# Seven quarter products for eight in two token-major products, and operand tiles at multiples of 512 bytes

## The chip, the core and the metric

The kernel runs on one core of one Trainium2 chip. Its time is the device time of one execution in microseconds; the median of the runs counts. TensorE (PE) does the matmuls, VectorE (DVE), ScalarE (ACT) and GpSimd (POOL) the elementwise work, and SyncE's queue (SP) issues nearly all DMAs.

## The reference

A trunk of two layers on 512 tokens of 1024 channels, in float32. Cut to what matters here:

```python
h = x
# layer 0: gMLP mixer
z = gelu(rmsnorm(h, g0) @ w_in)          # 1024 -> 4096
u, v = split(z)                          # 2048 columns each
s = spatial_mix(layernorm(v)) + b        # over tokens, in chunks of 128
h = h + (u * s) @ w_out
h = h + (silu(conv(hn @ w_gate)) * (hn @ w_up)) @ w_down
# layer 1: forgetting attention, 16 heads of 64
q, k, v, f = split(rmsnorm(h, g1) @ w_qkvf)
h = h + attention(q, k, v, cumsum(log_sigmoid(f + b_f))) @ w_o
h = h + (silu(conv(hn @ w_gate)) * (hn @ w_up)) @ w_down
out = rmsnorm(h, g_final)
```

The change concerns `v` of layer 0 (1024 by 2048 weights) and `v` of layer 1 (1024 by 1024).

## The kernel before

Every float32 product is made of three matmuls on halves: each operand is split into a rounded high half and the rest, and `triple` (L163 to L169) adds high by high, high by low and low by high into one PSUM bank. The residual stream `h` lies in SBUF channel-major, eight tiles of 128 channels by 512 tokens. `norm_split` makes the halves `xh`, `xl` of the scaled `h` of each tile (ACT L126, DVE L127); `norm_square` squares it on ACT and adds the squares up on GpSimd (L140, L141). The RMS factor per token is applied to the product's result, so a product may begin before the factor is there.

Weights stream in units of 128 by 1024 (512 KB) through SP's queue into `raw` (three buffers). For each unit ACT casts the high half `whi` (L112) and DVE subtracts to get the low half `wlo` (L113), two buffers each; `unit` and `fetch` keep two units ahead.

Two kinds of product use them. `gemm_fm` (channel-major output) takes weights as the stationary operand, 24 matmuls of 512 columns per unit. `gemm_tm` (L187 to L206, token-major output) has token blocks of x stationary and the weights moving: per group of 512 output columns four banks, four units, 24 matmuls of 512 columns per unit. In `gmlp` it makes v in four groups; the GELU (ACT L248) reads the banks, and `bn_stats` (DVE L249) follows. In `fox` it makes V in two groups, scaled into halves from the banks (L385, L386). `norm_end`, `norm_spread`, `gates`, `running_sums` and `spatial` hang on points inside these products.

At the start the first unit comes in two halves and x in quarters and then pairs of tiles, all on SP's queue, with `norm_split` of each pair behind it. The output products of gMLP and of both FFNs have products' inputs `z` (halves in 32 tiles); the down product's evacuation `add_to_h` (L210 to L220) adds four banks to `h`, splits them and squares them. The order on each engine is set by the tile framework's scheduler, from the order in which the code is written, its dependencies and its own cost table.

## Time and profile before

| | us |
|---|---|
| median of 3 runs | 1096.44 (1095.24 to 1096.6) |
| the profiled execution | 1095.16 |
| its span | 1093.4, granted clock 0.998 |
| PE busy | 1075.3 (98%) |
| DVE busy | 620.2 (57%) |
| ACT busy | 440.7 (40%) |
| POOL busy | 67.3 (6%) |

The span runs from the first to the last instruction; the profiled execution's own time is 1.8 us longer. Busy shares are means over the stages. In order of time these are: v product (5.14 to 101.84 us), u product (to 203.36), gMLP output (to 291.35), first FFN (to 467.34) and its down product (to 555.25), fox V (to 608.19), QK and attention, fox output, second FFN, and the last down product from 995.68.

### The profile page before, as it was taken

What the parts mean: (1) busy time and instruction counts of PE and PEld (TensorE: products, weight loads), DVE (VectorE), ACT (ScalarE), POOL (GpSimd) and SP (SyncE); (2) the same over time, 40 slices, a digit from 0 to 9 for tenths busy, and PEclk for the clock granted to TensorE, in tenths of its full rate; (3) what the DMA queues carried; (4) which work ended last, traced back from release to release, by engine and by line L of the source; (5) the groups of instructions that cost most, each with busy time, mean ns of one, the idle gap of its engine ahead of it and who ended that gap; (6) DMA issues with size and microseconds to landing.
All of it is one profiled execution on the core that took longest, in us unless ns stands there. A gap on an engine that the chain in (4) does not pass through costs nothing. (4 is left out here: it accounts for less than half of the span.)

```text
span 1093.4 us, 12918 instructions
## 1 busy us (share of the span) xinstructions
PE 1075.3 (98%) x5018; PEld 882.4 (81%) x5018; DVE 620.2 (57%) x1007; ACT 440.7 (40%) x706; POOL 67.3 (6%) x62
## 2 busy tenths in 40 slices
PE   7999999999999999999999999999999999999997
PEld 6878888888888888888887787777778888888886
DVE  5435856524555665545255588898665656655232
ACT  5332333323333433333133577777542433432232
POOL 6000000001200000001020000000021000000000
PEclk9999999999999999999999999999999999999999
DMA  6322222222222222222222211211222222232222
GB/s 237 109 84 97 86 89 78 86 95 96 90 95 97 97 97 97 97 97 97 97 97 81 81 61 44 77 40 53 84 77 97 97 97 96 82 111 87 89 95 77
DMA packets 28957, 99.44 MB, mean 91 GB/s; under 512 B 3488, under 2 KB 4256, under 8 KB 28896
## 3 DMA queue, kind: packets, MB, share of 16 engines
q1 hardware_dynamic: 28752, 98.52, 26.1%
q8 instruction: 39, 0.64, 0.2%
q14 instruction: 22, 0.18, 0.1%
q10 hardware_dynamic: 144, 0.10, 0.0%
HBM read 96.12 MB, written 2.10 MB: 90 GB/s over the span
## 5 line engine op out<-in xcount | busy, mean ns | idle before, releaser
L113 DVE TENSOR_TENSOR wlo<-raw,whi 128x1024 fp32r<-128x1024 f32 (+1 forms) x173 | 217.0, 1255 | 377.9 <-ACT whi L112 365.5
L112 ACT CAST whi<-raw 128x1024 fp32r<-128x1024 f32 (+1 forms) x173 | 180.8, 1045 | 457.9 <-PE psg L168 123.7
L167 PE MATMUL psg<-x,whi 128*128 128x512 f32 x336 | 136.6, 407 | 0.0
L169 PE MATMUL psg<-x,wlo 128*128 128x512 f32 x336 | 131.4, 391 | 0.0
L168 PE MATMUL psg<-x,whi 128*128 128x512 f32 x336 | 130.9, 390 | 0.0
L167 PE MATMUL pss<-x,whi 128*128 128x512 f32 x208 | 81.8, 393 | 0.0
L169 PE MATMUL pss<-x,wlo 128*128 128x512 f32 x208 | 81.0, 389 | 0.0
L168 PE MATMUL pss<-x,whi 128*128 128x512 f32 x208 | 80.9, 389 | 0.0
L169 PEld LDWEIGHTS psg<-x,wlo 128*128 128x128 f32 x336 | 63.1, 188 | 13.7
L167 PEld LDWEIGHTS psg<-x,whi 128*128 128x128 f32 x336 | 64.1, 191 | 11.2 <-issue 0.2
L168 PEld LDWEIGHTS psg<-x,whi 128*128 128x128 f32 x336 | 63.3, 188 | 11.4 <-issue 0.2
L141 POOL TENSOR_TENSOR tmp<-tmp,tmp 128x512 f32<-128x512 f32 x28 | 45.1, 1612 | 402.7 <-ACT tmp L140 401.2
L167 PE MATMUL psg<-z,whi 128*128 128x512 f32 x128 | 50.7, 397 | 0.0
L169 PE MATMUL psg<-z,wlo 128*128 128x512 f32 x128 | 50.3, 393 | 0.0
L168 PE MATMUL psg<-z,whi 128*128 128x512 f32 x128 | 49.9, 390 | 0.0
L168 PEld LDWEIGHTS pss<-x,whi 128*128 128x128 f32 x208 | 39.1, 188 | 8.2 <-issue 0.2
L169 PEld LDWEIGHTS pss<-x,wlo 128*128 128x128 f32 x208 | 39.0, 188 | 8.2
L167 PEld LDWEIGHTS pss<-x,whi 128*128 128x128 f32 x208 | 39.1, 188 | 8.1 <-issue 0.2
L167 PE MATMUL psa<-x,whi 128*128 128x512 f32 x112 | 44.1, 394 | 0.0
L169 PE MATMUL psb<-x,wlo 128*128 128x512 f32 x112 | 43.6, 389 | 0.0
L168 PE MATMUL psa<-x,whi 128*128 128x512 f32 x112 | 43.6, 389 | 0.0
L167 PE MATMUL psb<-x,whi 128*128 128x512 f32 x112 | 43.6, 389 | 0.0
(283 smaller groups left out, 2233.2 us busy)
## 6 DMA issues: line engine op xcount, KB each, us to landing
raw<-w SPq DMA_DIRECT2D x175, 512.0 KB
out<-v SPq DMA_DIRECT2D x8, 256.0 KB
h<-x SPq DMA_DIRECT2D x3, 512.0 KB
raw<-w SPq DMA_DIRECT2D x2, 256.0 KB
h<-x SPq DMA_DIRECT2D x4, 128.0 KB
pt<-ws SPq DMA_DIRECT2D x1, 512.0 KB
pt<-bs SPq DMA_DIRECT2D x1, 512.0 KB
z<-cum SPq DMA_DIRECT2D x32, 8.0 KB
```

The lines of the kernel that those rows point to most:

```text
L112: nc.scalar.copy(out=hi, in_=src)
L113: nc.vector.tensor_tensor(out=lo, in0=src, in1=hi.bitcast(F32), op=ALU.subtract)
L141: nc.gpsimd.tensor_tensor(out=self.acc, in0=self.acc, in1=sq, op=ALU.add)
L167: self.nc.tensor.matmul(out, ah, bh, start=start, stop=False)
L168: self.nc.tensor.matmul(out, ah, bl, start=False, stop=False)
L169: self.nc.tensor.matmul(out, al, bh, start=False, stop=stop)
```

## The change

It brings in a class `Seven`: one step of a Strassen-Winograd scheme. For a group of 512 output columns, x is cut into halves of channels (even and odd tiles, `k = 2q` and `2q + 1`) and of tokens (0 to 255, 256 to 511), the weights into four quarters 11, 12, 21, 22 of one unit each. Instead of eight quarter products there are seven, numbered 1 to 7: 1 and 2 take plain quarters of x and of the weights; 5, 6 and 7 take sums `S` of x quarters and differences of weight quarters; 4 takes a plain quarter of x with a difference, 3 takes a sum with quarter 22. One product is 24 matmuls of 256 columns into one bank (two token blocks, four `q`, three matmuls).

Around it: `sums` makes the S of one q (ACT scales h, DVE three subtractions and one combined operation of 256 columns each, then halves of four quarters); `diff` makes weight differences on DVE, 128 by 1024, four per group; `product` adds the seven results up into output quarters in SBUF (DVE, and an ACT copy for product 1). For a plain quarter with `added` (seven times in gMLP, twice in fox) the low half is not subtracted by DVE: ACT writes the negated high half, and a DMA issued by GpSimd adds the weights to it from memory. The GELU and fox's scaling read SBUF instead of the bank. gMLP runs 28 products, fox 14. Groups 0 and 1 are interleaved by `START`. In fox, the sums of q = 0 and 1 are made in the first group of the preceding down product.

The tiles in SBUF are laid out anew: before, z stood at 320 bytes past a multiple of 512, v at 128, pt at 320, hl and cum at 64; x and the weight halves at 0. After it all stand at 0. The tiles z, S, `rawx`, `dhi` and `wf` share a pool that is closed and opened again between stages. x comes in quarters of 128 KB, four of them on ACT's queue and twelve on SP's; two small loads move to the front of SP's queue. `quarters` packs the weights on the host in place of `blocks` for the two products.

The diff, cut to its core:

```diff
+class Seven:
+    QUARTER = {"11": 0, "12": 1, "21": 2, "22": 3}
+    def __init__(self, k, base, out, placed, done, added, wide):
+        self.k, self.base, self.out, self.placed, self.done = k, base, out, placed, done
+        self.added, self.wide = added, wide
+        self.raw, self.made, self.forms, self.part, self.ready = {}, {}, {}, {}, set()
+    def load(self, g, n):
+        if (g, n) not in self.raw:
+            k = self.k
+            tag, bufs = ("raw", 3) if n in ("11", "21") and not self.wide(g) else ("rawx", 5)
+            self.raw[g, n] = t = k.sb(tag, bufs, [P, 1024])
+            k.nc.sync.dma_start(out=t, in_=k.ins["w"][self.base + 4 * g + self.QUARTER[n]])
+        return self.raw[g, n]
+    def diff(self, g, t):
+        if (g, t) not in self.made:
+            tt = self.k.nc.vector.tensor_tensor
+            if t == 1:
+                b = self.k.sb("rawx", 5, [P, 1024])
+                tt(out=b, in0=self.load(g, "11"), in1=self.load(g, "12"), op=ALU.subtract)
+            elif t == 3:
+                self.diff(g, 1)
+                b = self.load(g, "12")
+                tt(out=b, in0=self.load(g, "22"), in1=b, op=ALU.subtract)
+            elif t == 2:
+                t3, b = self.diff(g, 3), self.load(g, "11")
+                tt(out=b, in0=t3, in1=b, op=ALU.add)
+            else:
+                t2, b = self.diff(g, 2), self.load(g, "21")
+                tt(out=b, in0=b, in1=t2, op=ALU.subtract)
+            self.made[g, t] = b
+        return self.made[g, t]
+    def prepare(self, g, p):
+        if (g, p) in self.ready:
+            return
+        self.ready.add((g, p))
+        k = self.k
+        n = {1: "11", 2: "21", 3: "22"}.get(p)
+        src = self.load(g, n) if n else self.diff(g, {5: 1, 6: 2, 7: 3, 4: 4}[p])
+        if n and self.added(g, p):
+            hi, lo = k.sb("dhi", 3, [P, 1024], F32R), k.sb("hl", 3, [P, 1024], F32R)
+            k.nc.scalar.copy(out=hi, in_=src)
+            k.nc.scalar.activation(out=lo, in_=hi.bitcast(F32), func=AF.Copy, scale=-1.0)
+            k.nc.gpsimd.dma_start(out=lo, in_=k.ins["w"][self.base + 4 * g + self.QUARTER[n]].bitcast(F32R), accum_op=ALU.add)
+        else:
+            hi, lo = k.sb("whi", 2, [P, 1024], F32R), k.sb("wlo", 2, [P, 1024], F32R)
+            k.split(hi, lo, src)
+        self.forms[g, p] = hi, lo
+    def product(self, g, p):
+        mm, tt = self.k.nc.tensor.matmul, self.k.nc.vector.tensor_tensor
+        bank = self.k.bank()
+        hi, lo = self.forms.pop((g, p))
+        for i in range(2):
+            for q in range(4):
+                ah, al = self.k.operand(p, q)
+                t, c = slice(i * P, (i + 1) * P), slice(q * 256, (q + 1) * 256)
+                o = bank[:, i * 256 : (i + 1) * 256]
+                mm(o, ah[:, t], hi[:, c], start=q == 0, stop=False)
+                mm(o, ah[:, t], lo[:, c], start=False, stop=False)
+                mm(o, al[:, t], hi[:, c], start=False, stop=q == 3)
+        part = self.part
+        def quarter(src, i, j):
+            a, b = (v.rearrange("p (i c) -> p i c", i=2) for v in (bank, src))
+            tt(out=self.out(g, i, j), in0=a, in1=b, op=ALU.add)
+            if self.placed:
+                self.placed(g, i, j)
+        if p == 1:
+            part[g, 1] = self.k.tmp()
+            self.k.nc.scalar.copy(out=part[g, 1], in_=bank)
+        elif p in (6, 7):
+            part[g, p] = self.k.tmp()
+            tt(out=part[g, p], in0=bank, in1=part[g, {6: 1, 7: 6}[p]], op=ALU.add)
+        elif p == 2:
+            quarter(part[g, 1], 0, 0)
+        elif p == 4:
+            quarter(part[g, 7], 1, 0)
+        elif p == 5:
+            quarter(part[g, 7], 1, 1)
+            tt(out=part[g, 6], in0=bank, in1=part[g, 6], op=ALU.add)
+        else:
+            quarter(part[g, 6], 0, 1)
+    def run(self, order, hook):
+        k = self.k
+        left = {}
+        for n, (g, p) in enumerate(order):
+            hook(n)
+            used = {"w": 0, "d": 0}
+            for m in range(n, min(n + 9, len(order))):
+                c = "d" if order[m][1] < 4 and self.added(*order[m]) else "w"
+                if used[c] < 2 + (c == "d"):
+                    self.prepare(*order[m])
+                used[c] += 1
+            while n >= len(order) - 2 and used["w"] + len(k.ahead) < 2 and k.iu < k.limit:
+                k.fetch()
+            self.product(g, p)
+            left[g] = left.get(g, 7) - 1
+            if left[g] == 0:
+                self.done(g)
+    START = [(0, 1), (0, 2), (1, 1), (1, 2)] + [(g, p) for g in (0, 1) for p in (6, 7, 5, 4, 3)]
...
+    TOP = ("z", "S", "rawx", "dhi", "wf")
+    def open_top(self):
+        self.top_cm = self.tc.tile_pool(name=self.name("top"), bufs=1)
+        self.top = self.top_cm.__enter__()
+    def close_top(self):
...
+        if self.iu == self.limit and self.coming:
+            for p in (1, 2)[: 2 - len(self.ahead)]:
+                self.coming.prepare(0, p)
...
+    def sums(self, q, gcol, tiles):
+        nc = self.nc
+        hi, lo = (t.rearrange("p (n t) -> p n t", n=4) for t in tiles)
+        f = [self.tmp().rearrange("p (n t) -> p n t", n=2) for _ in range(2)]
+        for j in range(2):
+            k = 2 * q + j
+            nc.scalar.activation(out=f[j], in_=self.h[k].rearrange("p (n t) -> p n t", n=2), func=AF.Copy,
+                                 scale=self.vec[:, gcol + k : gcol + k + 1])
+        a1, a2, b1, b2 = (f[n // 2][:, n % 2] for n in range(4))
+        nc.vector.tensor_tensor(out=a1, in0=a1, in1=a2, op=ALU.subtract)
+        nc.vector.scalar_tensor_tensor(out=a2, in0=a2, scalar=-1.0, in1=b2, op0=ALU.mult, op1=ALU.subtract)
+        nc.vector.tensor_tensor(out=b2, in0=b2, in1=a1, op=ALU.subtract)
+        nc.vector.tensor_tensor(out=b1, in0=b1, in1=b2, op=ALU.subtract)
+        for j in (1, 0):
+            self.split(hi[:, 2 * j : 2 * j + 2], lo[:, 2 * j : 2 * j + 2], f[j])
+        self.S[q] = hi, lo
+    def operand(self, p, q):
+        if p in (1, 2, 4):
+            k = 2 * q + (p != 1)
+            t = slice(256, 512) if p == 4 else slice(0, 256)
+            return self.xh[k][:, t], self.xl[k][:, t]
+        hi, lo = self.S[q]
+        n = {7: 0, 5: 1, 3: 2, 6: 3}[p]
+        return hi[:, n], lo[:, n]
...
+                if tiles and m % 2 and g == 0:
+                    self.sums(k // 2, gcol, tiles(k // 2))
...
+        def hook(n):
+            if n in (1, 2, 3):
+                for q in {1: (0, 1), 2: (2,), 3: (3,)}[n]:
+                    self.sums(q, V_MIX, [self.sb("S", 8, [P, 1024], F32R) for _ in range(2)])
+            elif n in (5, 6):
+                for k in range(n - 5, KD, 2):
+                    self.norm_part(k, V_MIX, slice(256, 512))
+            elif n == 7:
+                for k in range(KD):
+                    self.norm_square(k)
+            elif n == 11:
+                self.norm_end()
+            elif n == 12:
+                self.norm_spread()
+            elif n == 18:
+                self.spatial()
...
+        w = Seven(self, 0, lambda g, i, j: v[g][:, 2 * i : 2 * i + 2, j * 256 : (j + 1) * 256], None, gelu,
+                  lambda g, p: g >= 2 or (p == 3 and g == 1), lambda g: g == 1)
+        self.begin(w)
+        w.run(w.START + [(g, p) for g in (2, 3) for p in (1, 2, 6, 7, 5, 4, 3)], hook)
+        self.close_top()
+        self.open_top()
...
-        self.gemm_tm((self.xh, self.xl), KD, 4, evac_v, each_v)
...
+        def scaled(g, i, j):
+            t = at.pop((g, i, j)).rearrange("p (i h d) -> p i h d", i=2, d=HD)
+            o = 8 * g + 4 * j
+            for n in range(2):
+                r = self.r4[:, 2 * i + n : 2 * i + n + 1]
+                vh, vl = (V[2 * i + n][:, o : o + 4, c] for c in (slice(0, HD), slice(HD, P)))
+                nc.scalar.activation(out=vh, in_=t[:, n], func=AF.Copy, scale=r)
+                nc.vector.scalar_tensor_tensor(out=vl, in0=t[:, n], scalar=r, in1=vh.bitcast(F32), op0=ALU.mult, op1=ALU.subtract)
+        return Seven(self, 96, out, placed, lambda g: None, lambda g, p: p == 3, lambda g: g == 1)
...
+        def hook(n):
+            if n == 0:
+                for q in (2, 3):
+                    self.sums(q, V_MIX + 8, [self.sb("S", 4, [P, 1024], F32R) for _ in range(2)])
+                self.iu, self.limit, self.coming = 104, NU - 4, None
+            elif n == 3:
                 self.norm_end()
+                self.acc = None
+            elif n == 4:
                 self.norm_spread()
                 self.gates()
+            elif n == 8:
                 self.running_sums()
...
-        self.gemm_tm(x, KD, 2, evac_v, each_v)
+        w.run(w.START, hook)
+        self.close_top()
+        self.open_top()
...
+    def begin(self, w):
+        nc = self.nc
+        for _ in range(KD):
+            self.xh.append(self.sb("x", 16, [P, T], F32R))
+            self.xl.append(self.sb("x", 16, [P, T], F32R))
+        def quarter(j, t, eng):
+            for q in range(KD // 2):
+                eng.dma_start(out=self.hb[q][:, j, t], in_=self.ins["x"][:, 2 * q + j, t])
+        half = [slice(0, 256), slice(256, 512)]
+        for j, n in enumerate(("11", "21")):
+            w.load(0, n)
+            quarter(j, half[0], nc.scalar if j == 0 else nc.sync)
+            w.prepare(0, 1 + j)
+            for k in range(j, KD, 2):
+                self.norm_part(k, V_MIX, half[0])
+        quarter(0, half[1], nc.sync)
+        quarter(1, half[1], nc.sync)
+        for g, n in ((1, "11"), (1, "21"), (0, "12"), (0, "22")):
+            w.load(g, n)
...
+            spare = {q: [self.sb("pt", 3, [P, 1280], F32R)[:, 0:1024],
+                         (self.sb("pt", 3, [P, 1280], F32R)[:, 0:1024] if q == 0 else self.sb("hl", 3, [P, 1024], F32R))]
+                     for q in range(2)}
+            self.run(self.gemm_fm((self.zh, self.zl), KE, 2, self.add_to_h(V_MIX + 8, lambda q: spare[q])))
+            self.close_top()
```

How rows move, at three places. Names: `psa`, `psb`, `psg`, `pss` are PSUM banks, `S` the sums, `wlo` and `whi` weight halves, `tmp` buffers of 512 columns.

First place, TensorE at the start, where products on sums begin. Before, the fourth unit of v's first group goes over to the fifth, the first of the second group:

```order
L167 MATMUL pss_196<-whi_253,x_135 128x512
L168 MATMUL pss_196<-wlo_254,x_135 128x512
L169 MATMUL pss_196<-whi_253,x_136 128x512
L167 MATMUL psa_311<-whi_283,x_89 128x512
L168 MATMUL psa_311<-wlo_284,x_89 128x512
L169 MATMUL psa_311<-whi_283,x_90 128x512
```

Both units are plain weight halves (`whi`, `wlo`) with plain x.

With the change, product 2 of group 1 ends and product 6 of group 0 (in `psa_373`) begins:

```order
L117 MATMUL pss_343<-wlo_291,x_137 128x256
L118 MATMUL pss_343<-whi_290,x_138 128x256
L116 MATMUL psa_373<-whi_339,S_218 128x256
L116 MATMUL psb_419<-whi_369,S_218 128x256
L117 MATMUL psa_373<-wlo_340,S_218 128x256
L118 MATMUL psa_373<-whi_339,S_219 128x256
L116 MATMUL psa_373<-whi_339,S_232 128x256
```

After 96 matmuls of 256 columns (products 1 and 2 of groups 0 and 1) come the first that read sums (`S_218`, `S_232`) and halves of weight differences (`whi_339`, `wlo_340`).

Second place, DVE at the start. Before, from the last pair of x tiles to the halves of the third to fifth unit:

```order
L127 SCALAR_TENSOR_TENSOR x_132<-h_7_78,vec_79,x_131 128x512
L127 SCALAR_TENSOR_TENSOR x_136<-h_7_78,vec_79,x_135 128x512
L113 TENSOR_TENSOR wlo_224<-raw_221,whi_223 128x1024
L113 TENSOR_TENSOR wlo_254<-raw_251,whi_253 128x1024
L113 TENSOR_TENSOR wlo_284<-raw_281,whi_283 128x1024
```

Between x and the stream of unit halves nothing else stands on DVE.

With the change, the twelve rows that end with the low half for product 6 of group 0:

```order
L247 TENSOR_TENSOR S_277<-tmp_279,S_276 128x512
L247 TENSOR_TENSOR S_277<-tmp_278,S_276 128x512
L286 SCALAR_TENSOR_TENSOR tmp_323<-tmp_323,tmp_324 128x256
L79 TENSOR_TENSOR rawx_187<-rawx_189,rawx_187 128x1024
L287 TENSOR_TENSOR tmp_324<-tmp_324,tmp_323 128x256
L82 TENSOR_TENSOR raw_139<-rawx_187,raw_139 128x1024
L288 TENSOR_TENSOR tmp_324<-tmp_324 128x256
L123 TENSOR_TENSOR v_115<-pss_343,tmp_319 128x2x256
L273 SCALAR_TENSOR_TENSOR x_136<-h_23_94,vec_65,x_135 128x256
L247 TENSOR_TENSOR S_322<-tmp_323,S_321 128x512
L247 TENSOR_TENSOR S_322<-tmp_324,S_321 128x512
L247 TENSOR_TENSOR wlo_340<-raw_139,whi_339 128x1024
```

`S_277` and `S_322` are low halves of sums, `rawx_187` and `raw_139` weight differences (L79, L82), `v_115` an output quarter. Ahead of these stand 21 more rows from the first sum on, so 33 in all.

Third place, DVE where the down product of layer 0 ends and fox V begins. Before, the last two adds to `h`, three splits and the halves of two units:

```order
L216 TENSOR_TENSOR h_7_78<-psg_3589,h_7_78 128x512
L127 SCALAR_TENSOR_TENSOR x_3838<-h_6_77,vec_79,x_3837 128x512
L216 TENSOR_TENSOR h_7_78<-psg_3590,h_7_78 128x512
L127 SCALAR_TENSOR_TENSOR x_3843<-h_7_78,vec_79,x_3842 128x512
L113 TENSOR_TENSOR wlo_3878<-raw_3875,whi_3877 128x1024
L127 SCALAR_TENSOR_TENSOR x_3848<-h_7_78,vec_79,x_3847 128x512
L113 TENSOR_TENSOR wlo_3908<-raw_3905,whi_3907 128x1024
```

The halves follow the splits at once.

With the change, between the last split of h (`x_4388`) and the half `wlo_4482` for product 1 of group 1 there are the sums of q = 2 and 3, a difference and a quarter:

```order
L285 TENSOR_TENSOR tmp_4427<-tmp_4427 128x256
L288 TENSOR_TENSOR tmp_4414<-tmp_4414 128x256
L247 TENSOR_TENSOR S_4412<-tmp_4413,S_4411 128x512
L286 SCALAR_TENSOR_TENSOR tmp_4427<-tmp_4427,tmp_4428 128x256
L247 TENSOR_TENSOR S_4412<-tmp_4414,S_4411 128x512
L287 TENSOR_TENSOR tmp_4428<-tmp_4428,tmp_4427 128x256
L288 TENSOR_TENSOR tmp_4428<-tmp_4428 128x256
L75 TENSOR_TENSOR rawx_4569<-raw_4341,rawx_4570 128x1024
L247 TENSOR_TENSOR S_4426<-tmp_4427,S_4425 128x512
L247 TENSOR_TENSOR S_4426<-tmp_4428,S_4425 128x512
L123 TENSOR_TENSOR tmp_4510<-pss_4485,tmp_4477 128x512
L247 TENSOR_TENSOR wlo_4482<-rawx_4479,whi_4481 128x1024
```

Three more rows of the first of these sums stand ahead of the ones shown. The half for that product stands fourteen rows behind the last split.

## Rows read from the trace of the kernel before

**Rows 1.** The page, busy time of each engine.
```profile
PE 1075.3 (98%) x5018; PEld 882.4 (81%) x5018; DVE 620.2 (57%) x1007; ACT 440.7 (40%) x706; POOL 67.3 (6%) x62
```

**Rows 2.** Windows: stretch in us, its length, busy us of each engine (instructions), granted clock.
```profile
0.00:101.84 101.84, 96.30 (x416) 77.22 (x417) 45.60 (x62) 40.41 (x56) 17.56 (x22) 1.00 0.39 136
5.14:33.00 27.86, 23.87 (x99) 18.25 (x100) 17.16 (x16) 14.26 (x23) 16.40 (x15) 1.00 0.67 243
555.25:608.19 52.94, 52.94 (x248) 42.97 (x246) 27.41 (x54) 18.06 (x25) 5.52 (x4) 1.00 0.25 83
```

**Rows 3.** Timeline of PE: start us, us, line, operation, idle before and its releaser.
```profile
22.36 0.50 PE L168 MATMUL psg<-wlo,x 128*128 128x512 f32 x1 [2.39 <-DVE wlo L113]
...
101.84 0.39 PE L167 MATMUL psa<-x,whi 128*128 128x512 f32 x1
```

**Rows 4.** Timeline of PE, 102 rows apart, then eight rows apart.
```profile
69.66 0.39 PE L169 MATMUL pss<-whi,x 128*128 128x512 f32 x1
...
92.78 0.39 PE L169 MATMUL psg<-whi,x 128*128 128x512 f32 x1
...
1085.79 0.28 PE L167 MATMUL psg<-x,z 128*128 128x256 f32 x1
...
1086.69 0.28 PE L169 MATMUL psg<-x,z 128*128 128x256 f32 x1
```

**Rows 5.** Groups by form: DVE, and ScalarE's cast: busy us, mean ns, idle before.
```profile
L113 DVE TENSOR_TENSOR wlo<-raw,whi 128x1024 fp32r<-128x1024 f32 x171 | 215.6, 1262 | 372.2 <-ACT whi L112 359.8 <-PE psb L272 12.2
...
L127 DVE SCALAR_TENSOR_TENSOR x<-h,vec,x 128x256 fp32r<-128x256 f32 x4 | 1.8, 480 | 0.4 <-ACT x L126 0.4
...
L112 ACT CAST whi<-raw 128x1024 fp32r<-128x1024 f32 x171 | 179.5, 1050 | 456.2 <-PE psg L168 123.7 <-PE pss L168 117.0 <-PE psb L168 103.7
```

**Rows 6.** Timeline of DVE, in the first 20 us and around 553 us.
```profile
14.07 6.03 DVE L127 SCALAR_TENSOR_TENSOR x<-h,vec,x 128x512 fp32r<-128x512 f32 x4
...
551.95 0.68 DVE L216 TENSOR_TENSOR h<-psa,h 128x512 f32<-128x512 f32 x1
...
553.43 0.75 DVE L127 SCALAR_TENSOR_TENSOR x<-h,vec,x 128x512 fp32r<-128x512 f32 x1
554.10 0.68 DVE L216 TENSOR_TENSOR h<-psg,h 128x512 f32<-128x512 f32 x1
554.70 1.21 DVE L127 SCALAR_TENSOR_TENSOR x<-h,vec,x 128x512 fp32r<-128x512 f32 x1
```

**Rows 7.** Timeline of GpSimd (POOL), the adds of the squares.
```profile
14.85 6.38 POOL L141 TENSOR_TENSOR tmp<-tmp,tmp 128x512 f32<-128x512 f32 x4
```

**Rows 8.** Windows, the start: the last column is DMA in GB/s.
```profile
0.00:4.00 4.00, 2.94 (x14) 2.94 (x15) 0.00 (x0) 1.49 (x2) 1.16 (x7) 1.00 0.52 142
4.00:8.00 4.00, 3.57 (x18) 2.69 (x17) 1.87 (x4) 3.01 (x6) 0.00 (x0) 1.00 0.86 277
8.00:20.00 12.00, 10.38 (x42) 7.27 (x40) 10.96 (x10) 10.74 (x18) 10.55 (x10) 1.00 0.80 312
```

**Rows 9.** Windows for the clock: start, an early hole, the end.
```profile
2.00:3.00 1.00, 1.00 (x7) 1.00 (x6) 0.00 (x0) 0.73 (x2) 0.00 (x0) 1.00 0.84 222
4.00:4.50 0.50, 0.50 (x6) 0.50 (x5) 0.00 (x0) 0.44 (x1) 0.00 (x0) 1.00 0.60 184
...
20.00:22.30 2.30, 0.00 (x0) 0.00 (x0) 2.30 (x3) 0.16 (x1) 2.23 (x3) 1.00 0.00 0
...
1090.00:1091.00 1.00, 0.00 (x0) 0.00 (x0) 0.00 (x0) 0.00 (x0) 0.00 (x0) 0.50 0.53 199
```

**Rows 10.** Windows of PE alone (z moving, z stationary), then attention's PE rows.
```profile
203.36:291.35 87.99, 87.99 (x387) 1.00 0.28 96
...
995.68:1040.56 44.88, 44.88 (x195) 1.00 0.27 94
...
696.61 0.40 PE L169 MATMUL psg<-x,wlo 128*128 128x512 f32 x1
...
698.69 0.40 PE L169 MATMUL psg<-x,wlo 128*128 128x512 f32 x1
```

132 lines of the change are left out of this document (65 added, 67 removed).

## The prediction

> **What bounds the kernel now.** I read the page's engine lines first, then windows over the stages that change, then TensorE's rows there, then the costs on VectorE (DVE). TensorE is busy 1075.3 of 1093.4 us, DVE 620.2 [rows 1], so over the whole run TensorE sets the time. By stage it is the same: in the v product with what precedes it (to 101.84 us) TensorE works 96.30 us, DVE 45.60; in fox's V product (555.25 to 608.19) TensorE works all 52.94, DVE 27.41 [rows 2]. The v product starts at 5.14 and ends at 101.84, where the next bank begins, with early holes, the longest 2.39 us behind a weight half that DVE owed [rows 3]. So the question is how much work the change hands to DVE in just these two stages, and when.
>
> **TensorE's saving.** A 512-column matmul on the operands at multiples of 512 bytes takes 23.12 us / 102 = 0.2267 us, a 256-column one 0.90 / 8 = 0.1125 us, each with weights of its own [rows 4]; I take half of 0.2267, 0.1133. v: 384 x 0.2267 = 87.0 becomes 28 x 24 x 0.1133 = 76.2. V: 192 x 0.2267 = 43.5 becomes 14 x 24 x 0.1133 = 38.1. Fully fed TensorE would save 10.9 + 5.4 = 16.3 us; one product is 24 x 0.1133 = 2.72 us.
>
> **DVE's new work.** Costs by form: 128x1024 with two inputs 1.26, the scalar form of 128x256 0.48 [rows 5]. Consecutive operations start 0.08 closer than they last: 0.67 apart for a 0.75, 0.60 for a 0.68 [rows 6]. So back to back I count 1.15 for 1024 columns (the mean holds stretched ones), 0.61 and (scalar form) 0.67 for 512, 0.40 for the scalar form of 256 and, a little less as at 512, 0.36 for the plain one. While GpSimd adds squares (four in 6.38 us [rows 7]), four DVE operations with two inputs in SBUF took 6.03 instead of 4 x 0.67, and another 1.21 instead of 0.75 [rows 6]: (6.03 - 2.68) / 4 = 0.84 us per add. The chain of seven adds, now between products 4 and 11, so costs DVE about 5.7 us. The Trainium skill ("SBUF — State Buffer", section "Who interferes with whom") says that of two such operations the second to issue is blocked for the whole of the other; by it the sum would be that of rival 5. The rows show about half of such a block, and I keep to them.
>
> *v stage.* Group 0's first two products need halves of x, which arrive while DMA has moved 0.57 MB by 4 us, 1.68 by 8 and then 312 GB/s [rows 8]: the 2 MB of x and the 1 MB of the first two units are in at about 12.2 us. DVE's first 13 rows cost 6.7 us and lie in that time. Product (0,6) (group 0, product 6; the first on sums S, as the first place shows) then needs all of DVE's next 33 rows, to wlo_340 (second place shown with the change): six of 1024 columns, ten of 512, seventeen of 256, 19.3 us. So it starts at 12.2 + 19.3 = 31.5 at best; with the hand-offs to ScalarE in that alternating chain I take **33 us**. TensorE has by then only four products, 10.9 us of work. Then come five products (13.6 us) for which DVE owes ten operations of 1024 and ten smaller, 16.8 us, plus the 5.7: 22.5. Not all stands ahead of (1,6), the rest is queued up; I take (1,6) 7 us late, at 33 + 13.6 + 7 = 53.6. The remaining 19 products are 51.7 us and 1.5 of small matmuls; DVE's rows for that time sum to 49.9, 94% of it, so I add 2 us of stalls: the end is 108.8 against 101.84, **+7.0**. Bounds: fed without a stall after 33 us, 33 + 24 x 2.72 + 1.5 = 99.8, -2; with twice the blocking and 3 us more, +11. I take a value nearer the upper end, because all of DVE's rows here make 6.7 + 19.3 + 16.8 + 5.7 + 49.9 = 98.4 us, as long as the whole stage was (96.7).
>
> *fox V.* The first add of the stage starts 3.3 us before it, at 551.95 [rows 6]. From there to the half that (1,1) needs, DVE has nine operations of 512, four scalar ones of 512, three of 1024 and eight of 256 (third place): 14.6 us, and four adds x 0.84 = 3.3 more: 14.6 us into the stage. TensorE has two products until then, done at about 7, since the first already needs an x of the last add (before, that x was needed three units later). Then twelve products, 32.6 us; 9.4 us of gates and sums (52.94 - 43.52), of which 2 fit in the hole; and stalls before (0,6), (0,7) and (1,6), together 6, for the same reason as above: 14.6 + 32.6 + 7.4 + 6 = 60.6, **+7.7**. Bounds +2 (no further stalls, and only the hole remains) and +11.
>
> *Sums in the down product's first group.* They are queued on DVE among that group's adds, while the next group wants halves; TensorE is fed two units ahead. 0 to 2, I take **+1**.
>
> *Clock.* It stayed full (2.4 GHz) over 2.3 us without a matmul, at 20 us, and stood at 0.50 (1.2 GHz) at 1090, after the last matmul [rows 9]. The new holes are longer than any in the rows: most of 33 - 12.2 less two products, some 15 us in pieces, before (0,6); 7 in fox. Warm-up pieces ran 7 in a us from 2.0, and 6 in half a us from 4.0 [rows 9]: some 3 us at half pace after a start, a loss of 1.5 each time, an estimate from these rows. Two holes: **+3**, bounds 0 and 6.
>
> *Alignment.* Products with z as operand now take 87.99 / 384 = 0.2291 us where z moves, and 44.88 / 192 = 0.2338 where it is stationary [rows 10], against 0.2267 for x and weights [rows 4]; z stands at 320 mod 512. If that is why, the gMLP output product gains 0.95, the down product (alike) 0.9, fox's output 0.5, the last down product 1.4 in its first group and 1.0 behind. QK matmuls during attention run at 2.08 / 9 = 0.231 [rows 10] although their own operands are aligned; the pt, hl and cum tiles near them are not: up to 2.7. Ends 0 and -7.4; I take **-6**, since the z rows are split from the x rows by nothing else I see. The gelu that reads SBUF now, the small weight and bias loads moved to the front of SP's queue and ScalarE's extra copies cost nothing: ScalarE's cast is 1.05 us a unit [rows 5], under DVE's 1.26, and it follows DVE.
>
> Sum: 7.0 + 7.7 + 1 + 3 - 6 = **+12.7**, against the profiled execution's 1095.16: 1107.9, say **1108**. That execution is 1.3 us below the median shown (1096.44).
>
> **Rivals.**
> 1. *DVE is late once only (the other side).* If the chain before (0,6) ends by 31.5 and the two buffers of weight halves carry the rest, v breaks even, fox pays +2, no clock is lost, and the alignment gives all 7.4: -5.4, 1090. It decides at (1,6): before 48 us this case holds, after 51 mine. For it: from 5.14 to 33 us DVE works only 17.16 us before the change [rows 2], and the u stage after it can take late statistics. Against: 98.4 us of rows in 96.7. Chance 0.20.
> 2. *Fully fed.* -16.3 - 6: 1073. Against: TensorE's four products and DVE's 33 rows. 0.04.
> 3. *Alignment is worth nothing.* The QK rows at 0.231 with aligned operands say that something else slows them, and it may be so for z: 1108 + 6 = 1114. The Trainium skill (same page and section) has TensorE wait for no other engine's access, and gives alignment no price; by it this case holds. The z rows speak for some effect of place. 0.12.
> 4. *Late low halves by GpSimd's DMA.* Nine low halves are now built by a DMA that GpSimd issues and that adds into a ScalarE result; no row of before shows one. They queue behind GpSimd's adds, 1.6 us each. At nothing they are in the sum; at 2 us for each, 18 us, half of it hidden: 1117; with a DVE that is also blocked, 1122. 0.12.
> 5. *DVE stands still for every whole add.* An add is 6.38 / 4 = 1.6 us; seven cost 11.2 instead of 5.7, fox's four 6.4 instead of 3.3: +8.6, 1117. Against: the 0.84 per add worked out above. 0.05.
>
> **How the numbers follow.** My forecast (1100 to 1113) has 0.40. A measurement here can tell 0.2%, 2.2 us. Faster by more: rivals 1 and 2, 0.24; within: the edge between rival 1 and mine, 0.07; slower: the rest, 0.69. The range 1088 to 1122 leaves out rival 2, the worst of 4 and the far ends of the bounds.
>
> **What would show it.** In the changed profile: the first matmul on S at 33 us and the first of (1,6) at about 54, the releaser of the holes before them DVE; u's first matmul near 109; fox V some 61 us long with a hole of about 7 us ending at its third product; clock below full in the 10 us after such a hole; matmuls on z at 0.2267 us. I am wrong if v ends before 100, or if z's pace stays at 0.229, or if the holes are released by GpSimd's queue.

## The result, and the profile after

The changed kernel takes 1125.19 us (median of 4 runs, 1122.01 to 1127.27) against 1096.52: ratio 1.0263, interval 1.0238 to 1.0287. It is slower, as forecast, but by 28.7 us where the forecast had 12.7 above the profiled execution, and beyond the range's end of 1122. The profiled execution took 1122.01 with a span of 1120.3 and a granted clock of 0.982; before it was 1095.16, 1093.4 and 0.998. Below, spans and stages are those of the profiled executions. The changed kernel's four runs spread over 5.3 us and the profiled one is the fastest of them, so a difference of one or two us against its stages is not clear of that spread.

The page of the changed kernel, first lines (engines, then the granted clock in 40 slices):

```profile
PE 1077.1 (96%) x5450; PEld 909.3 (81%) x5450; DVE 702.4 (63%) x1143; ACT 491.1 (44%) x784; POOL 78.7 (7%) x71
...
PEclk8889999999999999999998999999999999999999
```

TensorE is busy about as long as before [rows 1]. What is new is 25 us more of waiting (span less busy time, 43.2 us against 18.1), 17 of it before 80 us and 7 in fox V; stretches at the lower clock count as busy. A table of stages, from the first matmul of each to that of the next (the third kernel is experiment 1):

| stage | before | changed | layout alone |
|---|---|---|---|
| first matmul of v at | 5.14 | 8.09 | 5.12 |
| v product | 96.70 | 116.25 | 96.41 |
| u product | 101.52 | 101.45 | 101.42 |
| gMLP output | 87.99 | 87.14 | 87.13 |
| first FFN | 175.98 | 175.93 | 175.93 |
| its down product | 87.91 | 87.57 | 87.04 |
| fox V | 52.94 | 60.13 | 52.78 |
| QK, attention | 148.77 | 148.76 | 148.76 |
| fox output | 61.11 | 61.00 | 60.94 |
| second FFN | 177.62 | 177.61 | 177.61 |
| last down product, to its last matmul | 91.01 | 89.50 | 89.51 |

So v ends 22.5 us later (124.34 against 101.84), fox V is 7.2 us longer, and the layout gives back 3. The windows of the changed kernel in v, where in [rows 2] TensorE worked 96.30 of 101.84 us (columns: busy us of PE, PEld, DVE, ACT, POOL with instructions, then the granted clock):

```profile
0.00:20.00 20.00, 13.55 (x66) 12.29 (x66) 9.94 (x20) 12.66 (x23) 2.60 (x14) 0.83 0.85 290
20.00:40.00 20.00, 11.44 (x62) 10.45 (x63) 18.65 (x33) 11.94 (x20) 4.74 (x1) 0.72 0.17 65
40.00:60.00 20.00, 14.51 (x108) 13.90 (x106) 15.09 (x15) 13.27 (x18) 11.89 (x7) 0.93 0.65 180
60.00:80.00 20.00, 17.74 (x111) 16.77 (x112) 16.25 (x28) 7.41 (x10) 5.11 (x4) 0.76 0.30 79
80.00:100.00 20.00, 20.00 (x159) 19.04 (x158) 17.77 (x23) 14.38 (x19) 2.58 (x3) 1.00 0.58 126
```

Up to 80 us TensorE works 13.5, 11.4, 14.5 and 17.7 of each 20 us and the clock's mean falls to 0.72; DVE is at 18.65 of 20 in the second window. From 80 us on TensorE never waits. Its rows at the holes, to be held against [rows 3]:

```profile
8.09 0.40 PE L116 MATMUL psg<-whi,x 128*128 128x256 f32 x1 [2.93 <-ACT whi L246]
...
34.76 0.58 PE L116 MATMUL psa<-whi,S 128*128 128x256 f32 x1 [5.24 <-ACT whi L246]
...
37.35 0.58 PE L117 MATMUL psa<-wlo,S 128*128 128x256 f32 x1 [0.54 <-DVE wlo L247]
37.73 0.42 PE L118 MATMUL psa<-whi,S 128*128 128x256 f32 x1
...
38.16 0.41 PE L117 MATMUL psa<-wlo,S 128*128 128x256 f32 x1
...
55.04 0.28 PE L118 MATMUL pss<-whi,S 128*128 128x256 f32 x1
60.95 0.58 PE L116 MATMUL pss<-whi,S 128*128 128x256 f32 x1 [5.63 <-ACT whi L246]
...
64.52 1.87 PE L319 MATMUL psa<-ones,tmp 128*128 128x1 f32 x8 [1.28 <-POOL tmp L312]
...
66.83 0.41 PE L117 MATMUL pss<-wlo,S 128*128 128x256 f32 x1
...
124.34 0.40 PE L338 MATMUL psa<-x,whi 128*128 128x512 f32 x1
```

Product (0,6) has its first matmul at 34.76 and goes on in earnest only at 37.35, behind its low half. The two rows behind it start 0.43 apart, two matmuls at 0.215: half rate. Group 0's last matmul starts at 55.04. (1,6) gets one matmul at 60.95 and the rest from 66.83. In between, eight small matmuls of `norm_end` (L319) stand in TensorE's queue; they read the sum of squares and wait for GpSimd's last add.

### The profile page after: what moved, and what is told of

Its sections match the earlier page's. It is cut to its first block, busy times and chain, and to the rows that moved or that the text cites. A ratio compares the mean times of both kernels' runs of the same rounds, so it can differ in the third digit from the quotient of the medians.

```text
span 1120.3 us, 14058 instructions
## 1 busy us (share of the span) xinstructions
PE 1077.1 (96%) x5450; PEld 909.3 (81%) x5450; DVE 702.4 (63%) x1143; ACT 491.1 (44%) x784; POOL 78.7 (7%) x71
## 5 line engine op out<-in xcount | busy, mean ns | idle before, releaser
L247 DVE TENSOR_TENSOR wlo<-raw,whi 128x1024 fp32r<-128x1024 f32 x160 | 199.8, 1249 | 314.1 <-ACT whi L246 301.8
L246 ACT CAST whi<-raw 128x1024 fp32r<-128x1024 f32 x160 | 168.0, 1050 | 395.4 <-PE pss L339 116.3
L312 POOL TENSOR_TENSOR tmp<-tmp,tmp 128x512 f32<-128x512 f32 x28 | 48.6, 1735 | 503.0 <-ACT tmp L311 282.1
L340 PEld LDWEIGHTS psg<-x,wlo 128*128 128x128 f32 x336 | 63.1, 188 | 13.5
L340 PE MATMUL psa<-x,wlo 128*128 128x512 f32 x112 | 43.6, 389 | 0.0
```

Of the source, the lines that this page charges most:

```text
L246: nc.scalar.copy(out=hi, in_=src)
L247: nc.vector.tensor_tensor(out=lo, in0=src, in1=hi.bitcast(F32), op=ALU.subtract)
L312: nc.gpsimd.tensor_tensor(out=self.acc, in0=self.acc, in1=sq, op=ALU.add)
L340: self.nc.tensor.matmul(out, al, bh, start=False, stop=stop)
```

## The experiments

The theory after the result: v is late because DVE and ScalarE owe halves, and the chain of seven squares and adds makes it worse than I had reckoned; rivals are the clock (holes cost more at half rate than they last), the buffers of raw quarters, and the pace of short matmuls.

**1. Layout alone.** The kernel before with small tiles first and a pad, so that all operand tiles stand at multiples of 512:

```diff
...
+            self.sb("tc", 2, [P, P])
+            self.sb("pad", 1, [P, 80])
...
```

> The kernel before with nothing but the new layout of tiles in SBUF (every operand tile at a multiple of 512 bytes). My forecast gave this 6 us: 1090.5 against 1096.5. The changed kernel's own stages say less: gMLP output 87.99 to 87.14, fox output 61.11 to 61.00, last down product 91.01 to 89.50, attention 148.77 to 148.76, so 3.3 with the down product free of the sums, that is 1093.2. If place is worth nothing: 1096.5. The 256-column matmuls of the last down product, 0.113 us before and 0.120 in part of the changed kernel, should stand at 0.120 if the place of z makes them slower, at 0.113 if something else in the change does.

1092.63 us against 1095.27, ratio 0.9974 (0.9964 to 0.9984): faster than both kernels. Windows of TensorE over the two products in which z moves:

```profile
202.95:290.08 87.13, 87.13 (x387) 1.00 0.28 97
466.02:553.06 87.04, 87.04 (x386) 1.00 0.28 97
```

Two matmuls of 256 columns with z stationary in the same kernel, 14 rows apart:

```profile
1080.98 0.28 PE L167 MATMUL psg<-x,z 128*128 128x256 f32 x1
...
1082.66 0.28 PE L169 MATMUL psg<-x,z 128*128 128x256 f32 x1
```

87.13 / 384 = 0.2269 us, the pace of x [rows 4, 10]. The gain is half of the 6 us that I took: attention did not move. And the 256-column matmuls became slower: 1.68 / 14 = 0.120, where [rows 4] had 0.1125. So the aligned place helps 512 columns and costs 256.

**2. The old v product in the changed kernel.** Start and v with eight quarter products, fox V with seven.

```diff
-        w.run(w.START + [(g, p) for g in (2, 3) for p in (1, 2, 6, 7, 5, 4, 3)], hook)
...
+        self.gemm_tm((self.xh, self.xl), KD, 4, evac_v, each_v)
...
```

> The changed kernel with layer 0's v product and the start as before (eight quarter products, 512 columns); fox V keeps its seven, the layout stays. If the costs of the two products add: 96.7 us for v again, fox V about 60, in all 1096.5 + 7.2 - 2.9 = 1101. If layer 0's v did its damage by something that the rest shares (clock, layout), v stays long: 1115 or more. If fox V is only slow because it follows a disturbed start: 1094.

1100.73 us, ratio 1.0053 (1.0039 to 1.0066); v 97.88, fox V 60.47. The costs add, and fox V is slow by itself.

**3. Idle time filled.** Dummy matmuls on a finished tile before (1,1), (0,6) and (1,6), 28 warm-up matmuls:

```diff
+DUMMY = {2: 14, 4: 36, 9: 34}
...
+                for _ in range(DUMMY[n]):
+                    nc.tensor.matmul(pw[:, 0:P], d, d, start=True, stop=True)
...
-            for _ in range(9):
+            for _ in range(28):
```

> The changed kernel with idle TensorE time filled: 28 instead of 9 warm-up matmuls, and dummy matmuls of 128 columns (14, 36 and 34) between products (0,2) and (1,1), (1,2) and (0,6), (0,3) and (1,6). Theory clock: about 95 matmuls of v ran at 0.213 us instead of 0.120, so 9 to 10 us come back, v ends near 115. Theory DVE: what runs ahead of (0,6) and (1,6) waits for DVE anyway; only half-pace matmuls behind them count, 2 to 4 us, v ends near 121, and the granted clock is 1.00 from 5 to 70 us all the same.

1124.78 us, ratio 1.0272: no gain, and v ends at 126.31. The clock was 1.00 up to 60 us, and (1,6) ran in full from 59.83, 7 us earlier. There the matmuls of `norm_end` came behind it, from 65.56. But the scheduler, which counts the dummies, had moved rows: a difference that waits for a load stood ahead of (1,5)'s half. Rows of TensorE and DVE there:

```profile
72.92 0.58 PE L118 MATMUL psb<-wlo,S 128*128 128x256 f32 x1 [6.18 <-DVE wlo L248]
```

And its DVE:

```profile
61.92 1.21 DVE L76 TENSOR_TENSOR rawx<-raw,rawx 128x1024 f32<-128x1024 f32 x1
68.65 1.23 DVE L80 TENSOR_TENSOR rawx<-rawx,rawx 128x1024 f32<-128x1024 f32 x1 [5.51 <-DMA rawx<-w]
...
71.65 1.22 DVE L248 TENSOR_TENSOR wlo<-rawx,whi 128x1024 fp32r<-128x1024 f32 x1
```

TensorE waits 6 us for a half (row 71.65) that stands behind L80, which waited 5.51 us for its load. v ends beyond what either theory expected, so the test does not tell them apart; experiment 9 repeats it with rows in place.

**4. Six buffers for raw quarters** (two instead of three for `dhi`, since SBUF is full):

```diff
-            tag, bufs = ("raw", 3) if n in ("11", "21") and not self.wide(g) else ("rawx", 5)
+            tag, bufs = ("raw", 3) if n in ("11", "21") and not self.wide(g) else ("rawx", 6)
...
-                if used[c] < 2 + (c == "d"):
+                if used[c] < 2:
```

> The changed kernel with six rawx buffers instead of five (dhi two instead of three, and two added forms ahead instead of three). Theory: group 1's differences wait for the slot that product (0,3)'s split frees at 52 us, so the hole of 5.9 us before (1,6) and the half clock behind it hang on that slot; with a slot more they start near 44 us, (1,6) follows (0,3) within 1 us, v ends 7 to 11 us earlier, at 114 to 117. Rival: DVE's total work sets it, or the squares' adds on GpSimd do; the hole only moves, v ends at 121 to 124.

1132.26 us, ratio 1.0352: slower still, and v ends at 130.17, outside both expectations. Group 1's differences did start at 43.52 instead of 52.76, and (1,6) still began only at 58.27. ScalarE's queue shows why (start, us, operation, idle before and releaser):

```profile
52.23 0.63 ACT L311 ACTIVATE tmp<-h 128x512 f32<-128x512 f32 x1 [1.69 <-POOL tmp L312]
54.45 0.63 ACT L311 ACTIVATE tmp<-h 128x512 f32<-128x512 f32 x1 [1.59 <-POOL tmp L312]
56.65 0.63 ACT L311 ACTIVATE tmp<-h 128x512 f32<-128x512 f32 x1 [1.57 <-POOL tmp L312]
57.19 1.98 ACT L246 CAST whi<-rawx 128x1024 fp32r<-128x1024 f32 x2
```

And GpSimd of that kernel:

```profile
46.17 14.86 POOL L312 TENSOR_TENSOR tmp<-tmp,tmp 128x512 f32<-128x512 f32 x7 [7.55 <-ACT tmp L311]
```

The casts for (1,6) (L246) stand behind the last square, and each square waits for an add on GpSimd to give its buffer back; the seven adds take 14.86 us. The difference that (1,6) needs was ready at 53.28, its cast began 3.9 us later. So the five slots had held the differences back, but theirs was not the last wait. The two `dhi` buffers then opened new holes (2.1 and 4.0 us, both ended by the DMA into `hl`), so the run's total says nothing on the slots.

**5. Without the seven adds.**

```diff
-            nc.gpsimd.tensor_tensor(out=self.acc, in0=self.acc, in1=sq, op=ALU.add)
+            if not skip:
+                nc.gpsimd.tensor_tensor(out=self.acc, in0=self.acc, in1=sq, op=ALU.add)
```

> The changed kernel without the seven GpSimd adds of squares in layer 0's v stage (the squares themselves stay on ScalarE; the norm of layer 0's mixer is then that of the first tile's squares alone). Theory: the adds, 2.1 us each, hold ScalarE's queue by the square buffers, with (1,6)'s cast behind them, and stretch four differences and a split on DVE. Without them the differences run from 52.8 to 56.8, cast and split to 59, (1,6) in full at 59 instead of 66.8: v ends at 116 to 118, 1115 to 1118 in all. If the holes come from the five rawx slots or from the clock alone: v ends at 122 to 124.

1116.72 us, ratio 1.0191 (1.0175 to 1.0206); v ends at 118.26, 6.1 us earlier. (1,6) ran in full from 62.67, 4.2 us earlier, not from 59: the scheduler had also moved the squares ahead of the cast for (0,3), so the differences began at 54.75 instead of 52.76. They last 1.23 each, where the changed kernel shows on DVE:

```profile
52.76 1.71 DVE L75 TENSOR_TENSOR rawx<-rawx,rawx 128x1024 f32<-128x1024 f32 x1
54.51 2.19 DVE L79 TENSOR_TENSOR rawx<-rawx,rawx 128x1024 f32<-128x1024 f32 x1
56.63 0.68 DVE L123 TENSOR_TENSOR v<-pss,tmp 128x512 f32<-128x512 f32 x1
57.23 1.68 DVE L82 TENSOR_TENSOR rawx<-rawx,rawx 128x1024 f32<-128x1024 f32 x1
58.95 2.18 DVE L85 TENSOR_TENSOR rawx<-rawx,rawx 128x1024 f32<-128x1024 f32 x1
61.05 2.30 DVE L247 TENSOR_TENSOR wlo<-rawx,whi 128x1024 fp32r<-128x1024 f32 x1
```

ScalarE of the changed kernel, same stretch:

```profile
53.43 0.63 ACT L311 ACTIVATE tmp<-h 128x512 f32<-128x512 f32 x1 [1.78 <-POOL tmp L312]
...
55.66 0.63 ACT L311 ACTIVATE tmp<-h 128x512 f32<-128x512 f32 x1 [0.65 <-POOL tmp L312]
57.87 1.15 ACT L311 ACTIVATE tmp<-h 128x512 f32<-128x512 f32 x2 [1.58 <-POOL tmp L312]
58.92 1.04 ACT L100 ACTIVATE hl<-dhi 128x1024 fp32r<-128x1024 f32 x1
59.87 1.98 ACT L246 CAST whi<-rawx 128x1024 fp32r<-128x1024 f32 x2
```

And its GpSimd, the seven adds in one row:

```profile
49.61 14.86 POOL L312 TENSOR_TENSOR tmp<-tmp,tmp 128x512 f32<-128x512 f32 x7
```

Two of these seven on their own, and an add of the kernel before with DVE idle beside it:

```profile
53.48 2.15 POOL L312 TENSOR_TENSOR tmp<-tmp,tmp 128x512 f32<-128x512 f32 x1
55.70 2.13 POOL L312 TENSOR_TENSOR tmp<-tmp,tmp 128x512 f32<-128x512 f32 x1
...
23.66 1.28 POOL L141 TENSOR_TENSOR tmp<-tmp,tmp 128x512 f32<-128x512 f32 x1
```

TensorE of the kernel without adds, where `norm_end` has nothing to wait for:

```profile
60.95 0.95 PE L320 MATMUL psa<-ones,tmp 128*128 128x1 f32 x8
```

Three things are to be seen. On DVE five two-input operations take 1.71, 2.19, 1.68, 2.18 and 2.30 instead of 1.22 (a sixth, at 63.27, takes 2.28), and they take turns with the adds. The add of 53.48 ends at 55.63, 1.16 us after the difference before it (52.76 + 1.71 = 54.47); the difference of 54.51 ends at 56.70, 1.07 after that add; the add of 55.70 ends at 57.83, 1.13 after that difference. Each gets on only when the other is done. On ScalarE the cast for (1,6) starts at 59.87, 1.0 us after its difference is there (57.23 + 1.68 = 58.91), behind squares that wait 1.8, 0.7 and 1.6 us for GpSimd. On TensorE (1,6) stands still until 66.83 behind the matmuls of `norm_end`, which wait for the last add until 64.52, while its low half is done at 61.05 + 2.30 = 63.35.

**6. The adds on DVE.**

```diff
-                    self.norm_square(k)
+                    self.norm_square(k, nc.vector)
```

> The changed kernel with these seven adds on DVE instead of GpSimd. DVE has 7 x 0.61 = 4.3 us more; no operation is stretched, ScalarE's squares wait for DVE only. Theory: (1,6) in full near 62, v ends at 118 to 121, 1118 to 1121 in all. If GpSimd's adds did no harm beyond DVE's time: slower than the changed kernel by up to 4 us.

1118.91 us, ratio 1.0211 (1.0196 to 1.0226), v ends at 121.08, (1,6) runs in full from 62.27. Seven more operations on the engine that is late are still better than the same adds beside it.

**7. Squares and adds after product 13.**

```diff
-            elif n == 7:
+            elif n == 13:
                 for k in range(KD):
                     self.norm_square(k)
-            elif n == 11:
+            elif n == 18:
                 self.norm_end()
...
```

> The changed kernel with squares and adds after product 13 instead of 7, the norm's end after 18, the GELU of groups 0 and 1 with that of group 2. Theory: the hole before (1,6) shrinks as in the kernel without adds, and a smaller one opens behind, since DVE is 89% busy from 80 to 100 us: v ends at 116 to 121. If the adds cost what they cost wherever they stand: 124 as before.

1121.92 us, ratio 1.0236; v ends at 123.19, outside the 116 to 121 expected and 1.2 us before the changed kernel. The hole before (1,6) shrank, it ran in full from 59.91, with `norm_end` far behind it. Another hole came and the clock fell to a mean of 0.83 between 80 and 100:

```profile
89.00 0.58 PE L117 MATMUL pss<-hl,S 128*128 128x256 f32 x1 [2.87 <-DMA hl<-w]
```

It was not DVE that ended it, as the theory had it, but a low half that GpSimd's DMA builds: the DMA was issued at 81.40, right behind the seven adds, and landed at 88.96. The delay moved rather than went.

**8. S at other places.**

```diff
-                    self.sums(q, V_MIX, [self.sb("S", 8, [P, 1024], F32R) for _ in range(2)])
+                    self.sums(q, V_MIX, S[q])
...
+        for q, pad in enumerate((0, 16, 16, 48)):
+            if pad:
+                self.sb(f"Sp{q}", 1, [P, pad])
+            S.append([self.sb(f"S{q}", 2, [P, 1024], F32R) for _ in range(2)])
```

> The changed kernel with layer 0's sums S at 0, 64, 128 and 320 bytes past a multiple of 512 for q = 0, 1, 2, 3; nothing else moves. If it is the place of the stationary operand that sets the pace of 256-column matmuls (0.113 us with z at 320, 0.120 with z at 0), those on q = 1 to 3 stand at 0.113 and those on q = 0 at 0.120 in one kernel; some 2 us less in all. If it is anything else: 0.120 for all.

1123.12 us (two runs), v ends at 125.05: the 2 us expected in all did not show. The first matmuls of q = 0, 1, 2, 3 and again 0 in one product, three rows apart:

```profile
88.20 0.28 PE L116 MATMUL psa<-whi,S 128*128 128x256 f32 x1
...
88.56 0.28 PE L116 MATMUL psa<-whi,S 128*128 128x256 f32 x1
...
88.91 0.28 PE L116 MATMUL psa<-whi,S 128*128 128x256 f32 x1
...
89.27 0.28 PE L116 MATMUL psa<-whi,S 128*128 128x256 f32 x1
...
89.61 0.28 PE L116 MATMUL psa<-whi,S 128*128 128x256 f32 x1
```

0.36 / 3 = 0.120 us on q = 0, 0.34 / 3 = 0.113 on q = 3, which stands at 320. Over the full-rate products on S without a gap the means are 0.119, 0.119, 0.118 and 0.114 for q = 0, 1, 2 and 3, so 64 and 128 give next to nothing, against the expectation. In products on x, still aligned, it is 0.120. So the place of the stationary operand bears on the pace. It is not all: with all S at 320 (experiment 11) gaps stand at 0.113 in two products and at 0.118 in seven, and why is open.

**9. Idle time filled, rows in place.** Fewer dummies than in experiment 3; DVE, ScalarE and GpSimd keep the changed kernel's order.

```diff
-DUMMY = {2: 14, 4: 36, 9: 34}
+DUMMY = {2: 14, 4: 36, 9: 14}
```

> The first filling of idle time moved rows on DVE and ScalarE, and a new wait for a load took the gain. Here the dummies are fewer (28 warm-up matmuls, 14 before (1,1), 36 before (0,6), 14 before (1,6)), and the rows of every other engine keep the changed kernel's order. Theory: half clock lengthens product (0,1) and (1,1), whose bank copies stand in ScalarE's queue ahead of the sums, and the five products from (0,6) on; (0,6) in full 2 us earlier, the five 2 us shorter, (1,6) 4 to 7 us earlier, v ends at 117 to 120. If the clock only fills time in which DVE is late anyway: v ends at 123 to 124.

1120.03 us, ratio 1.0222 (1.0204 to 1.0239); v ends at 122.76, 1.6 us earlier and not at the 117 to 120 expected. Product (0,6) ran in full from 35.15, 2.2 us earlier, (1,6) from 62.88, 4 us earlier, again behind the matmuls of `norm_end`, which waited for GpSimd until 60.57. Later waits took back part of it. The clock was 1.00 to 40 us and then 0.94 and 0.81:

```profile
20.00:40.00 20.00, 18.81 (x159) 18.61 (x160) 20.00 (x32) 11.70 (x20) 1.54 (x1) 1.00 0.25 95
40.00:60.00 20.00, 15.32 (x119) 14.43 (x117) 16.68 (x14) 13.84 (x18) 15.68 (x9) 0.94 0.63 157
60.00:80.00 20.00, 19.30 (x128) 18.65 (x129) 15.39 (x29) 8.35 (x11) 1.32 (x2) 0.81 0.31 79
```

**10. Without adds, idle time filled.**

```diff
+DUMMY = {2: 14, 4: 36, 9: 16}
...
-                    self.norm_square(k)
+                    self.norm_square(k, True)
...
```

> The kernel without the seven GpSimd adds (the norm of layer 0's mixer is that of the first tile's squares alone), with idle time filled (28, 14, 36, 16), same order on the other engines. If adds and clock act apart: v ends 4 to 6 us before the 118.3 of the kernel without adds, at 112 to 114, all with granted clock 1.00. If both are one and the same delay of DVE: 117 to 118. What is left over 101.8 is then pace (28 x 24 x 0.0067 = 4.5 us) and DVE's own work.

1112.89 us, ratio 1.0156 (1.0139 to 1.0173); v ends at 114.68, 3.6 us before the kernel without adds, with the clock at 1.00 throughout. (1,6) ran in full from 59.03. So adds and clock are not one delay; together they take 9.7 us. Their shares are not fixed: filling idle time gained 3.6 us here and 1.6 with the adds in place (experiment 9).

**11. The best whole version with seven products.** Adds on DVE, filled idle time, S at 320:

```diff
+DUMMY = {2: 14, 4: 36, 9: 12}
...
+                    self.norm_square(k, nc.vector)
...
+        self.sb("Sp", 1, [P, 80])
...
```

> A version that computes all: the changed kernel with the seven adds on DVE, idle time filled (28, 14, 36, 12), and layer 0's S tiles at 320 bytes past a multiple of 512. From the parts: adds on DVE 121.1 for the end of v, filling 2 to 4 less, S 2 to 3 less: 114 to 117, 1112 to 1115 in all. Still slower than before.

1115.54 us, ratio 1.0181 (1.0162 to 1.0201), v ends at 117.61, a little above the 114 to 117 expected. Better than the change by some 9 us, still 20 behind before.

**12. Fox without its four adds**, on the kernel of experiment 2:

```diff
-                self.norm_square(4 * g + m)
+                self.norm_square(4 * g + m, g == 1 and gcol == V_MIX + 8)
```

> The kernel with the old v product and fox's seven, without the four GpSimd adds of squares of the last four tiles before fox V (the norm of fox then lacks these tiles' squares). DVE's rows between the last adds to h and the third product keep their order. In the changed kernel six of them last 3.0 us longer than the same forms elsewhere. If that is the adds: the third product starts 10.5 to 11 us into the stage instead of 13.5, fox V lasts 57 to 58 instead of 60.5, about 1098 in all. If the hole is ScalarE's queue or the loads: 60 again.

1098.31 us, ratio 1.0029 (1.0018 to 1.0040); fox V 57.76 instead of 60.47. The third product's first matmul, first in the changed kernel (stage from 576.43, here from 553.34), from TensorE's timeline:

```profile
589.95 0.58 PE L116 MATMUL psa<-whi,x 128*128 128x256 f32 x1 [6.36 <-ACT whi L246]
```

And without the four adds:

```profile
564.52 0.58 PE L116 MATMUL psa<-whi,x 128*128 128x256 f32 x1 [4.78 <-ACT whi L246]
```

It starts 11.2 us into the stage instead of 13.5. I take the hole that is left, 4.78 us, for DVE's and ScalarE's plain work on the sums; no run took that apart.

## Why the prediction was right and wrong

**The side was right, and the reason in part**: TensorE waits in the two stages for halves that DVE and ScalarE owe, and that costs more than the eighth product saves. Where and how long it waits came out otherwise. Term by term:

- *fox V*, +7.7: measured +7.2. A hole of 6.4 us that ends at the third product, 13.5 us into the stage (forecast 14.6), with DVE busy 13.27 of the 13.52 us before it. Experiment 12 shows 2.7 us of it to be the four adds (forecast 3.3). That the rest fits is luck. The 6 us of stalls before (0,6), (0,7) and (1,6) did not come, TensorE is busy from the third product on:

```profile
589.95:636.57 46.62, 46.57 (x343) 44.32 (x344) 41.30 (x81) 22.39 (x34) 0.84 (x1) 0.94 0.30 82
```

In their place stand 12 x 24 x 0.0067 = 1.9 us of a slower pace, which the forecast had at nothing, 2.0 us of matmuls at half rate (22 of them, some 0.093 us longer each), which it had at 1.5 in another term, and some 2 us of gates that did not fit in the hole.

- *Sums in the down product*, +1: measured 87.57 against 87.04 without them, 0.5.
- *Alignment*, -6: measured some -3.4 by experiment 1's stages (0.85, 0.87, 0.17 and 1.5) and -2.6 in its medians. The z terms held; the 2.7 us for attention were wrong, 148.77 became 148.76. Rival 3, that place is worth nothing, fell too. The section of the Trainium skill that it drew on ("SBUF — State Buffer", "Who interferes with whom") says that TensorE waits for no other engine. No run here speaks against that; the place of a tile, for which the section has no price, had one in these runs.
- *v*, +7.0 with the start: measured +22.5. This is the step that failed, by 15.5 us. Its parts:

| | forecast | measured |
|---|---|---|
| (0,6) runs from | 33 | 37.35 |
| the next five products | 13.6 | 17.7 (to 55.04) |
| until (1,6) runs | 7 | 11.8 (to 66.83) |
| from there to the end | 55.2 | 57.5 |

The wrong sentence is "I take (1,6) 7 us late, at 33 + 13.6 + 7 = 53.6". I had counted DVE's work there (six stretched operations, 5.0 us over 1.22 each, where I took 5.7), but not who else waits for the adds, nor that they last 14.86 / 7 = 2.12 us each beside 1024-column operations, where [rows 7] had 1.6. TensorE's own queue is the dearest place: the matmuls of `norm_end` stand inside (1,6) and wait for the last add. Without the adds (1,6)'s first matmul came only 1.3 us earlier (59.69 for 60.95), its rest 4.2 (62.67 for 66.83). ScalarE's queue adds 1.0 us before the cast for (1,6), since its squares wait for GpSimd to free their buffers (3.9 with six buffers for raw quarters, experiment 4). The prediction named a hole released by GpSimd's queue as a sign of being wrong; the 1.28 us that end at 64.52 are one. Experiment 5 puts the adds at 6.1 us of the 22.5, net of the rows that moved with them.

Nor did DVE owe halves without a pause, as that sum has it. From 41.15 to 52.76 us it was busy 6.77 of 11.61, and group 1's first difference began only at 52.76, when the split of (0,3) had given a buffer of raw quarters back; with a sixth buffer it began at 43.52 (experiment 4). What this wait is worth is not shown, since that run had new holes of its own.

The second is "I take half of 0.2267, 0.1133". No row had a 256-column matmul with its stationary operand at a multiple of 512: the 0.1125 of [rows 4] was measured with z at 320, and the change moves every tile to 0. At the measured 0.120 the 28 products cost 28 x 24 x 0.0067 = 4.5 us more, fox's 14 another 2.2. I had weighed the two parts of the change apart, and one makes the other dearer.

The third is where the clock's cost lies. The forecast had +3 for two holes, one of them in fox; v alone lost 3.6 us by it (experiment 10 against 5). With idle time filled (0,6) ran in full 2.2 us earlier (experiment 9): the half-rate product (1,1) delays the bank copy that stands in ScalarE's queue ahead of the sums (ScalarE waits 1.41 us for it until 26.69 in the changed kernel, and it runs at 23.69 in experiment 9).

Together: of 124.34 us, 76.2 are the 28 products as the forecast priced them, so 48.1 are lost, where the forecast had 108.8 - 76.2 = 32.6:

| lost in v, us | forecast | measured | from |
|---|---|---|---|
| until (0,6) runs, but for its first four products | 33 - 10.9 = 22.1 | 35.15 - 10.9 = 24.3 | experiment 9 |
| adds and their queue | within the next row | 6.1 | experiment 5 |
| (1,6) late, small matmuls, stalls | 7 + 1.5 + 2 = 10.5 | 10.2 | what is left |
| pace of 256 columns, behind (0,6) | 0 | 3.9 | 24 x 24 x 0.0067 |
| clock | (1.5, summed apart) | 3.6 | experiment 10 |

So the step for the start was 2.2 us short with the clock full, and what the forecast took for (1,6) with its adds is needed without them. The adds, the pace and the clock are what it lacked. The row "what is left" is a difference: the wait for a buffer is in it, and no run took DVE's rows before (0,6) apart from the late load. The adds are taken at the clock as it was, the clock without the adds; in the other order the shares would be 8.1 and 1.6.

**Rivals.** 1 (late once only) was the other side and lost at the place named: (1,6) came after 51 us. 2 lost at the same place. 4, late low halves by GpSimd's DMA: in the changed kernel no hole in v ends on one; with fewer buffers (experiment 4) two did, with late adds (experiment 7) two, of 0.86 and 2.87 us, and in experiment 11 one of 0.6. 5, DVE stands still for every whole add: its price was wrong, its mechanism was not. In experiment 5's rows a two-input operation ends 1.07 us after the add ends, and an add some 1.15 after the operation. The trace agrees here with the rule of the Trainium skill in that section, which I had set aside as double what the rows show. What DVE loses by an add is only the part in which it would have worked on such operands (0.5 to 1.1 us each time, 5.0 for the seven), and the 1.6 that rival 5 took for an add already held the add's own wait: alone it is 1.28. My 0.84 came from a row read wrongly: of its four operations the first ran its 0.74 us ahead of the adds, and the fourth add stretched the row behind, a weight half from 20.03, to 2.28. So it was 1.1 to 1.3 us an add there. That 5.7 came near the 5.0 measured is luck.

**The range** missed because its upper end rested on the v term's bound of +11, made from "twice the blocking", while the pace of short matmuls and the waits for the adds on TensorE and ScalarE had no bound at all.

## What to carry to other kernels

When work moves from TensorE to the engines that feed it, sum up that work per stage and then follow each in-order queue by name: a wait on a third engine (here GpSimd's adds, on ScalarE by a shared pool of buffers, on TensorE by the norm's small matmuls) holds everything that stands behind it, also what has nothing to do with it. A matmul's pace is read only from rows with the same width and the same placement; a layout that helps one width may cost another. Where only one part of a change gains, ship that part: the layout alone is 0.26% faster, while seven products lost in every form tried.
